# A macaron block on one core: the 7-product 2x2 block scheme in the first feed-forward as well

## The chip, the core and the metric

The kernel runs on one NeuronCore of a Trainium2 chip. The core has a matrix engine (PE, with a separate row PEld for its weight loads), a vector engine (DVE), a scalar engine (ACT), a general engine (POOL) and a queue engine (SP) that issues nearly all DMAs. Each engine works through its own list of instructions in order and waits on semaphores where an instruction needs another engine's result. The metric is the device time of one execution in microseconds (us).

## The reference, cut to what matters

One transformer-like layer on 256 tokens of 1024 features, in float32. Its first and last parts are feed-forward blocks of the same shape:

```python
def swiglu(h, w_in, w_down):              # h 256x1024, w_in 1024x5632, w_down 2816x1024
    gate, up = jnp.split(h @ w_in, 2, axis=-1)
    return (jax.nn.silu(gate) * up) @ w_down

h = rmsnorm(x, ffn1_pre_g[l])
x = x + 0.5 * rmsnorm(swiglu(h, ffn1_w_in[l], ffn1_w_down[l]), ffn1_post_g[l])
... # a gated linear recurrence, a causal attention, a cross-attention to a memory
h = rmsnorm(x, ffn2_pre_g[l])
x = x + 0.5 * rmsnorm(swiglu(h, ffn2_w_in[l], ffn2_w_down[l]), ffn2_post_g[l])
```

Only the order and the form in which `h @ w_in` is computed in the first block changes.

## The kernel before, in words

**Split products.** Every large product is made from two halves of each number: a rounded `hi` and the rest `lo = raw - hi`. A product takes three matmuls: hi by hi, hi by lo, lo by hi. So each weight tile of 128x1024 ("unit", 512 KB) is loaded into a buffer `raw` (four of them), ACT casts it to `hi` (L128) and DVE subtracts to get `lo` (L129); `hi` and `lo` have eight buffers each. A unit's load can start when a `raw` buffer is free, and its cast when a `hi`/`lo` pair is free.

**A feed-forward block** (`ffn`, L370 to L605) works through 11 chunks of 256 hidden columns. A chunk's projection has 4 weight units (512 columns, gate beside up) and, for each half of the tokens (`h`, 128 tokens), 8 blocks of 128 features by 3 matmuls: 48 matmuls of 128x512. `act_evac` then makes silu(gate)*up from PSUM (ACT L393/L395, DVE L401/L403). `flush` transposes a finished chunk on PE (L385) and splits it into `acts[c]`. `down(c, h)` multiplies it by 2 units of the down weight: 12 matmuls of 128x512 for a half, into four PSUM banks `acc`. Down products run one chunk or so behind the projections; the last three chunks' are left for the end (`STAG`). Then `post` normalises and adds, and the next stage begins.

**Where the two blocks differ.** The first block starts the kernel. Its chunks 0, 1 and 2 go through `act_first`, which uses each weight block for both token halves in turn, since the loads have only begun. The loads of the token matrix and of chunk 0's weights (`heads`, L611 to L616) use the four `raw` buffers and the two buffers `wide`. Its tokens `X1` carry no row scale; 1/rms enters in `act_evac` as `r2[h]`. The second block has tokens `X4` and at chunk 2 calls `mixed` (L265): `row_of` makes a row of the scales (two small matmuls on PE, L252), the tokens become full precision again and are multiplied by the row (`full`, L270 and L271), split anew (`N`), and four sums and differences of token blocks (`sums`, L280) are split as well. From chunk 3 on this block projects from `N`.

**`quad(c, done)`** (L408) computes two chunks together. The tokens are taken as 2x2 blocks (token half by even or odd feature block), the weights as 2x2 blocks (even or odd feature block by chunk), and the Winograd form of Strassen's scheme makes the 2x2 product with 7 block products in place of 8: 7 times 4 feature blocks times 3 matmuls, 84 in place of 96. In exchange DVE adds weight blocks (L436, L437, L439, L485) and both ACT and DVE split those sums (`two`, L414): 14 splits of 128x1024 for a pair of chunks in place of 8. The second chunk's raw weights go to `wide` (two buffers of two units). Four `down` calls stand between the products. In the kernel before, only the second block calls `quad`, for the pairs 5 with 6 and 8 with 9 (`QUADS`, L51 and L552).

**Buffers of one pool.** Token matrices, `acts`, `full`, `sums`, the weight sums (`sum`, L434) and the rows `grow` share a pool of 21 buffers of 4 KB per partition ("m4"). The next stage's token matrix `X2` (4 of them) is requested before the first block (L642).

**The order of the work** is made by a planner at build time. It reads the program in written order (that is the priority), keeps a simulated time for each engine, gives an engine the first instruction that is ready in its simulation, and gives buffers out as they come free. `after(n)` and `tc.issue_after` tie an instruction behind another one on its engine. On the chip the order of each engine, SP's included, is then fixed.

Of the kernel before, what the change touches and what calls it, by code (L numbers as in the profile page):

```python
# [16 lines left out]
P = 128  # L17
# [30 lines left out]

X_AT = 11

QUADS = (5, 8)  # L51


_ORDER = [
# [15 lines left out]
def block_kernel(ctx: ExitStack, tc: tile.TileContext, wts, head_in, gf_in, x_in, mem_in, memT_in, cols, rows, fbias, masks, out):  # L70
# [296 lines left out]
            queue.dma_start(out[h * P : (h + 1) * P, a:b], xh)  # L367


    def ffn(w_in, w_dn, X, r2, n_tok, i_row, first_half, second_half=None):  # L370

        acts = {}
        late = []
# [13 lines left out]

        mix = []

        def act_evac(ps, c, h):  # L390
# [5 lines left out]
            if c == NFF - 1 and h == 1 and not first_half:  # L396
                with tc.issue_after(silu.ins):
                    S.activation(warm, ones[:, 0:1], AF.Sqrt)
            a = sp.tile([P, FC], F32, tag="c1", name=nm("at"), bufs=7)
            if mix:  # L400
                V.tensor_tensor(out=a, in0=ps[:, FC:], in1=sg, op=ALU.mult)  # L401
            else:
                V.scalar_tensor_tensor(out=a, in0=ps[:, FC:], scalar=r2[h], in1=sg, op0=ALU.mult, op1=ALU.mult)  # L403
            ats[c, h] = a
            if (c, 1 - h) in ats:
                late.append(c)

        def quad(c, n_down):  # L408

            N, ((s1h, s1l), (s2h, s2l), (s3h, s3l), (s4h, s4l)) = mix[0]  # L410
            for k in (c, c + 1):
                acts[k] = m4([P, 2, 2, T], F32R, "act")

            def two(src):  # L414
                hi, lo = (p.rearrange("p (i n) -> p i n", i=2) for p in parts_of())
                split(hi, lo, src)
                return [(hi[:, i], lo[:, i]) for i in range(2)]

            B11, B21, wide, first, second_, fourth = ([] for _ in range(6))
            for q in range(2):  # L420
                W = wp.tile([P, 2, 2, 512], F32, tag="wide", name=nm("wide"), bufs=2)
                raws = []
                for i in range(2):
                    u = _AT[w_in] + 4 * c + 2 * q + i
                    raw = wp.tile([P, D], F32, tag="raw", name=nm("raw"), bufs=4)
                    loads.append(nc.sync.dma_start(raw, wts[u - 4]).ins)
                    loads.append(nc.sync.dma_start(W[:, i].rearrange("p j n -> p (j n)"), wts[u]).ins)
# [24 lines left out]
            def prod(ps, A, B, i, start, stop=False):  # L452
                (ah, al), (bh, bl) = A(i), B[i]
                MM(ps, ah, bh, start=start and i == 0, stop=False, skip_group_check=True)
                MM(ps, ah, bl, start=False, stop=False, skip_group_check=True)
                MM(ps, al, bh, start=False, stop=i == 3, skip_group_check=True)

            def prods(ps, A, B, start, stop=False):
                for i in range(4):
                    prod(ps, A, B, i, start, stop)  # L460

            def keep(ps):
                t = sp.tile([P, 512], F32, tag="z2", name=nm("keep"), bufs=3)
                S.copy(t, ps)
                return t

            b1, b2, b3 = mm(), mm(), trp()
# [4 lines left out]
            with tc.issue_after(summed):  # L472
                flush(n + L_ACT)
            p1 = keep(b1)
            prods(b2, F(s1h, s1l), T1, True)
            V.tensor_tensor(out=p1, in0=p1, in1=b3, op=ALU.add)
            act_evac(p1, c, 0)
            down(n_down, 0)
            T2 = two(second_[0]) + two(second_[1])
            prods(b1, F(s2h, s2l), T2, False)  # L480
            w = keep(b1)
            down(n_down, 1)
            T3 = []
# [6 lines left out]
            act_evac(v, c + 1, 1)  # L490
            down(n_down + 1, 0)
            T4 = two(fourth[0]) + two(fourth[1])
            prods(b1, X(1, 1), T4, False, True)
            act_evac(b1, c, 1)
            down(n_down + 1, 1)
            B22 = []
            for W in wide:
                B22 += two(W[:, :, 1])
            prods(b2, F(s4h, s4l), B22, False, True)
            V.tensor_tensor(out=w, in0=b2, in1=w, op=ALU.subtract)  # L500
            act_evac(w, c + 1, 0)

        def act_tok(c, h):
            ps = mm()
# [16 lines left out]
        def down(c, h, cols=((0, 512), (512, 1024))):  # L521
            act = acts[c]
            hs = slice(h * P, (h + 1) * P)
            for j in range(2):
                wh, wl = unit(w_dn, 2 * c + j)
                ah, al = act[:, 0, j, hs], act[:, 1, j, hs]
                for lo, up in cols:
                    for i, (a, w) in enumerate(((ah, wh), (ah, wl), (al, wh))):
                        MM(accs[h][lo // 512][:, lo % 512 : lo % 512 + up - lo], a, w[:, lo:up], start=(c == 0 and j == 0 and i == 0), stop=(c == NFF - 1 and j == 1 and i == 2))

        for c in range(n_tok):
            acts[c] = m4([P, 2, 2, T], F32R, "act")
        for h in range(2):
# [2 lines left out]
                act_tok(c, h)  # L536
            if h == 0 and n_tok:
                second_half(m)
        accs = None
        done = 0  # L540
        if callable(r2):
            outs = [act_first(c, acc) for c in range(2)]
# [6 lines left out]
        for c in range(n_tok, NFF):  # L549
            if c in acts:  # L550
                continue
            if not first_half and c in QUADS:  # L552
                quad(c, done)
                done += 2
                continue
# [7 lines left out]
            else:  # L563
                for h in range(2):
                    n = len(log)
                    act_tok(c, h)
                    if c == 2 or c > NFF - STAG + 1 or c - 2 in QUADS and not first_half:
                        flush(n + L_ACT)
            if c == NFF - 1:
                flush(n + L_ACT)  # L570
            if c == QUADS[0] - 3 and not first_half:
                mix.append(mixed(X, r2))
                X = mix[0][0]
            if c == (6 if first_half else 7):
# [6 lines left out]
            while done < min(c - 1, NFF - STAG):  # L581
                n = len(log)
                for h in range(2):
                    down(done, h)
                if first_half or c + 1 not in QUADS:
                    flush(n + L_ACT)
                done += 1
        left, right = (0, 512), (512, 1024)
        m = len(log)
        for cut in (left, right):  # L590
            for c in range(NFF - STAG, NFF):
                down(c, 0, (cut,))
        flush(m + L_ACT)
        post(accs[0], 0, grow, 0.5, not first_half)
        m = len(log)
        if first_half:
            for c in range(NFF - STAG, NFF):
                down(c, 1)
            first_half(m)
            post(accs[1], 1, grow, 0.5)  # L600
        else:
            for cut in (left, right):
                for c in range(NFF - STAG, NFF):
                    down(c, 1, (cut,))
            post_last(accs[1], 1, grow, 0.5)  # L605

# [32 lines left out]
            nc.sync.dma_start(fb_s, fbias)  # L639
# [620 lines left out]
```

## Time and profile before

| what | value |
| --- | --- |
| time, median of 3 runs | 795.22 us (795.21 to 795.88) |
| profiled execution, its own time | 795.3 us |
| profiled execution, its span of instructions | 793.5 us |
| PE busy | 784.3 us, 99% of the span |
| PEld, DVE, ACT busy | 86%, 71%, 55% |
| granted clock of PE, mean | 0.999 |
| bytes by DMA | 147.43 MB, mean 186 GB/s |

The profile page has six parts: busy time of each engine; the span in 40 slices of 19.8 us, with a digit for the busy tenths; DMA queues; the chain of work that ended last, followed back from the end; the costliest groups of instructions; DMA issues. Beside the page the trace answers views: windows (busy time of each engine in given stretches), a timeline of one engine (start, duration, engine, line, operation, tiles, count, and in brackets the idle time before it and what ended it), and the chain in order of time (start, length, what). All starts are us from the span's start. A matmul's busy time overlaps that of the next one, so the pace of matmuls is read from a stretch of the chain (length over count), not from an instruction's duration.

The first block runs from the start to about 192 us, the middle stages to about 602 us, the second block from there to the end.

### The profile page before, as it was taken

To read this page: it belongs to the slowest core of one execution; us is meant where nothing else is said; L and a number is where in the kernel's file an instruction comes from. 1 tells how busy PE (TensorE), PEld (TensorE's weight loads), DVE (VectorE), ACT (ScalarE), POOL (GpSimd) and SP (SyncE) were. 2 spreads that over 40 slices of the span, in tenths; PEclk is the share of its full clock that TensorE was granted. 3 is DMA by queue.
4 is the path that set the end of the run, shared out by engine and by line. 5 is a ranking of instruction groups with operands and counts; after the bars stand their busy time and mean duration, and the time that the engine had idled before them with its cause. 6 is when DMAs were issued, how large, how long until landed. Compare 5 with 4: busy or idle time off the path is not lost.

```text
span 793.5 us, 12866 instructions
## 1 busy us (share of the span) xinstructions
PE 784.3 (99%) x5048; PEld 679.2 (86%) x5048; DVE 565.0 (71%) x884; ACT 435.5 (55%) x659; POOL 9.2 (1%) x21
## 2 busy tenths in 40 slices
PE   9999999999999999999999999999999999999996
PEld 7888888888899999998888888999888888888885
DVE  6774545557767898578776665965758799978973
ACT  7654444546753446447675444754746655664751
POOL 0000000000000100100000000000000000000000
PEclk9999999999999999999999999999999999999999
DMA  9776755664555555653497755456454544473441
GB/s 347 250 256 207 220 194 159 189 209 160 162 184 143 178 174 157 211 195 120 141 313 270 234 172 198 137 183 212 133 176 143 185 161 163 162 256 113 154 159 53
DMA packets 43691, 147.43 MB, mean 186 GB/s; under 512 B 4840, under 2 KB 8304, under 8 KB 43632
## 3 DMA queue, kind: packets, MB, share of 16 engines
q1 hardware_dynamic: 43024, 144.92, 55.8%
q0 software_dynamic: 464, 1.58, 0.8%
q8 instruction: 39, 0.64, 0.3%
q14 instruction: 20, 0.16, 0.1%
q10 hardware_dynamic: 144, 0.13, 0.0%
HBM read 145.56 MB, written 1.06 MB: 185 GB/s over the span
## 4 chain that ended last, share of the span: by engine, by line
PE 98%; DMA 0%; DVE 0%; issue 0%; ACT 0%; DVEq 0%; ACTq 0%
PE mm L84 66%; PE acc L84 28%; PE tr L84 2%; PE tr L385 1%; PE tr L305 1%; DMA head<-in_head_dram 0%; PE tr L939 0%; PE tr L1028 0%; PE tr L1131 0%; DVEq L1258 0%; DVE xs L366 0%; DVE post L351 0%; ACT hi L629 0%; ACT hT L147 0%; ACT junk L234 0%
## 5 line engine op out<-in xcount | busy, mean ns | idle before, releaser
L129 DVE TENSOR_TENSOR lo<-raw,hi 128x1024 fp32r<-128x1024 f32 (+1 forms) x244 | 291.6, 1208 | 94.9 <-ACT hi L128 88.1
L128 ACT CAST hi<-raw 128x1024 fp32r<-128x1024 f32 (+1 forms) x244 | 249.3, 1037 | 138.8 <-PE mm L84 85.5
L84 PE MATMUL mm<-lo,hT 128*128 128x512 f32 (+1 forms) x544 | 208.6, 386 | 0.0
L84 PE MATMUL mm<-hi,hT 128*128 128x512 f32 (+1 forms) x544 | 208.4, 385 | 0.0
L84 PE MATMUL mm<-hi,lT 128*128 128x512 f32 (+1 forms) x544 | 207.3, 385 | 0.0
L84 PEld LDWEIGHTS mm<-hi,hT 128*128 128x128 f32 x544 | 102.2, 188 | 20.2 <-ACT hT L262 0.5
L84 PEld LDWEIGHTS mm<-hi,lT 128*128 128x128 f32 x544 | 102.1, 188 | 19.8 <-DVE lT L263 0.7
L84 PEld LDWEIGHTS mm<-lo,hT 128*128 128x128 f32 x544 | 102.0, 188 | 18.5
L84 PE MATMUL acc<-hi,act 128*128 128x512 f32 x352 | 112.7, 391 | 0.0
L84 PE MATMUL mm<-hT,hi 128*128 128x256 f32 x384 | 109.0, 284 | 0.1
L84 PE MATMUL mm<-hT,lo 128*128 128x256 f32 x384 | 109.0, 284 | 0.0
L84 PE MATMUL mm<-lT,hi 128*128 128x256 f32 x384 | 108.9, 284 | 0.0
L84 PEld LDWEIGHTS acc<-hi,act 128*128 128x128 f32 x352 | 66.1, 188 | 13.6 <-DVE act L148 0.2
L84 PEld LDWEIGHTS mm<-hT,hi 128*128 128x128 f32 x384 | 73.6, 192 | 0.4 <-issue 0.3
L84 PEld LDWEIGHTS mm<-hT,lo 128*128 128x128 f32 x384 | 73.6, 192 | 0.1
L84 PEld LDWEIGHTS mm<-lT,hi 128*128 128x128 f32 x384 | 73.6, 192 | 0.1
L84 PE MATMUL acc<-lo,act 128*128 128x512 f32 x176 | 69.6, 395 | 0.0
L84 PEld LDWEIGHTS acc<-lo,act 128*128 128x128 f32 x176 | 33.1, 188 | 6.4
L84 PE MATMUL acc<-hi,hT 128*128 128x512 f32 x96 | 35.6, 398 | 0.1
L84 PE MATMUL acc<-hi,lT 128*128 128x512 f32 x96 | 35.1, 392 | 0.0
L84 PE MATMUL acc<-lo,hT 128*128 128x512 f32 x96 | 34.9, 391 | 0.0
L395 ACT ACTIVATE sg<-mm,rstd 128x256 f32<-128x256 f32 x24 | 11.4, 476 | 36.6 <-PE mm L84 36.6
(233 smaller groups left out, 815.5 us busy)
## 6 DMA issues: line engine op xcount, KB each, us to landing
raw<-in_wts_dram SPq DMA_DIRECT2D x240, 512.0 KB, 4.5
raw<-in_gf_dram SPq DMA_DIRECT2D x12, 344.0 KB, 3.9
wide<-in_wts_dram SPq DMA_DIRECT2D x8, 512.0 KB, 6.0
head<-in_head_dram SPq DMA_DIRECT2D x8, 388.0 KB, 5.8
grow<-in_rows_dram SPq DMA_DIRECT2D x4, 512.0 KB, 6.0
xs<-in_x_dram SPq DMA_DIRECT2D x2, 512.0 KB, 8.6
cbm<-cd POOLq DMA_DIRECT2D x2, 512.0 KB, 7.9
brow<-in_rows_dram SPq DMA_DIRECT2D x4, 256.0 KB, 5.5
```

What stands on the lines that cost most here:

```text
L84: log.append(PE.matmul(*args, **kw).ins)
L128: S.copy(h, r)
L129: V.tensor_tensor(out=l, in0=r, in1=h.bitcast(F32), op=ALU.subtract)
L305: PE.transpose(ps[:, j * P : (j + 1) * P], src(kb), ident)
L385: PE.transpose(trv[:, j, h * P : (h + 1) * P], ats[c, h][:, j * P : (j + 1) * P], ident)
L395: silu = S.activation(sg, ps[:, :FC], AF.Silu, scale=r2[h])
```

## The change

A tuple of pairs is given to each block: `QUADS_1` for the first, `QUADS_2` for the second, both (5, 8). So the first block now also calls `mixed` at chunk 2, projects chunks 3 to 10 from `N`, and computes chunks 5 with 6 and 8 with 9 by `quad`. `X2` gets its buffers only at the end of the first block. The row `grow` is loaded at chunk 4 in both blocks (before: chunk 6 in the first, 7 in the second), since chunks 5 and 6 don't pass that line any more. The diff also adds branches for a pair that ends with the last chunk (`last`, `flush_half`, `done == NFF - 2`); with the pairs (5, 8) `quad` starts at 5 and 8, `NFF - 2` is 9, and none of them is taken. The branch `len(late) == 2` in `quad` isn't taken either: at both calls one finished chunk waits for its transposes.

```diff
-QUADS = (5, 8)
+QUADS_1 = (5, 8)
+QUADS_2 = (5, 8)
...
-    def ffn(w_in, w_dn, X, r2, n_tok, i_row, first_half, second_half=None):
+    def ffn(w_in, w_dn, X, r2, n_tok, i_row, quads, first_half, second_half=None):
...
+            if len(late) == 2:
+                flush(n + 4)
                 flush(n + L_ACT)
+            else:
+                with tc.issue_after(summed):
+                    flush(n + L_ACT)
...
-            if not first_half and c in QUADS:
+            if c in quads:
                 quad(c, done)
...
-                    if c == 2 or c > NFF - STAG + 1 or c - 2 in QUADS and not first_half:
+                    if c == 2 or c > NFF - STAG + 1 or c - 2 in quads:
                         flush(n + L_ACT)
...
-            if c == QUADS[0] - 3 and not first_half:
+            if quads and c == max(2, quads[0] - 3):
                 mix.append(mixed(X, r2))
                 X = mix[0][0]
-            if c == (6 if first_half else 7):
+            if grow is None and c >= 4:
                 grow = load_row(i_row)
...
-                if first_half or c + 1 not in QUADS:
+                if c + 1 not in quads:
                     flush(n + L_ACT)
...
-    X2 = Pair()
+    X2 = Pair(0)
...
-    ffn("f1_in", "f1_dn", X1, norm_1, 0, 0, lambda m: half(X2, r2, 0, G_MIX, m + L_F1))
+    def first(m):
+        X2.more()
+        X2.more()
+        half(X2, r2, 0, G_MIX, m + L_F1)
+
+    ffn("f1_in", "f1_dn", X1, norm_1, 0, 0, QUADS_1, first)
...
-    ffn("f2_in", "f2_dn", X4, r4, 2, 3, None, second)
+    ffn("f2_in", "f2_dn", X4, r4, 2, 3, QUADS_2, None, second)
```

More of the change, by code (lines that the diff above doesn't have):

```diff
@@ L388, in ffn, with flush_half @@
         mix = []
+        def flush_half(c, h, n):
+            trv = trp().rearrange("p (j t) -> p j t", j=2)[:, :, :P]
+            hs = slice(h * P, h * P + P)
+            with after(n):
+                for j in range(2):
+                    PE.transpose(trv[:, j], ats[c, h][:, j * P : (j + 1) * P], ident)
+                split(acts[c][:, 0, :, hs], acts[c][:, 1, :, hs], trv)
         def act_evac(ps, c, h):
@@ L395, in act_evac @@
                 silu = S.activation(sg, ps[:, :FC], AF.Silu, scale=r2[h])
-            if c == NFF - 1 and h == 1 and not first_half:
+            if c == NFF - 1 and (c, 1 - h) in ats and not first_half:
                 with tc.issue_after(silu.ins):
@@ L465, in keep @@
                 return t
+            last = c == NFF - 2
             b1, b2, b3 = mm(), mm(), trp()
@@ L471, in quad @@
                 prod(b3, X(0, 1), B21, i, True, True)
-            with tc.issue_after(summed):
+            if len(late) == 2:
+                flush(n + 4)
                 flush(n + L_ACT)
+            else:
+                with tc.issue_after(summed):
+                    flush(n + L_ACT)
             p1 = keep(b1)
@@ L481, in quad @@
             w = keep(b1)
+            n = len(log)
             down(n_down, 1)
+            if last:
+                flush_half(c, 0, n)
             T3 = []
@@ L490, in quad, with fourth_product, third_product @@
             act_evac(v, c + 1, 1)
+            n = len(log)
             down(n_down + 1, 0)
[L492 to L501, printed above, removed]
+            def fourth_product():
+                T4 = two(fourth[0]) + two(fourth[1])
+                prods(b1, X(1, 1), T4, False, True)
+                act_evac(b1, c, 1)
+            def third_product():
+                B22 = two(wide[0][:, :, 1]) + two(wide[1][:, :, 1])
+                prods(b2, F(s4h, s4l), B22, False, True)
+                V.tensor_tensor(out=w, in0=b2, in1=w, op=ALU.subtract)
+                act_evac(w, c + 1, 0)
+            if last:
+                down(n_down + 1, 1)
+                flush_half(c + 1, 1, n + L_ACT)
+                third_product()
+                n = len(log)
+                fourth_product()
+                flush_half(c + 1, 0, n + 12)
+            else:
+                fourth_product()
+                down(n_down + 1, 1)
+                third_product()
         def act_tok(c, h):
@@ L528, in down @@
                     for i, (a, w) in enumerate(((ah, wh), (ah, wl), (al, wh))):
-                        MM(accs[h][lo // 512][:, lo % 512 : lo % 512 + up - lo], a, w[:, lo:up], start=(c == 0 and j == 0 and i == 0), stop=(c == NFF - 1 and j == 1 and i == 2))
+                        MM(accs[h][lo // 512][:, lo % 512 : lo % 512 + up - lo], a, w[:, lo:up], start=(c == 0 and j == 0 and i == 0), stop=(c == (NFF - 2 if h and quads and quads[-1] == NFF - 2 else NFF - 1) and j == 1 and i == 2))
         for c in range(n_tok):
@@ L538, in ffn @@
                 second_half(m)
-        accs = None
+        accs = grow = None
         done = 0
@@ L589, in ffn @@
         m = len(log)
[L590 to L593, printed above, removed]
+        if done == NFF - 2:
+            for k in (NFF - 2, NFF - 1):
+                for cut in (left, right):
+                    down(k, 0, (cut,))
+            flush_half(NFF - 2, 1, m + L_Y)
+        else:
+            for cut in (left, right):
+                for c in range(done, NFF):
+                    down(c, 0, (cut,))
+            flush(m + L_ACT)
         post(accs[0], 0, grow, 0.5, not first_half)
         m = len(log)
+        ends = (NFF - 1, NFF - 2) if done == NFF - 2 else range(done, NFF)
         if first_half:
-            for c in range(NFF - STAG, NFF):
+            for c in ends:
                 down(c, 1)
@@ L602, in ffn @@
             for cut in (left, right):
-                for c in range(NFF - STAG, NFF):
+                for c in ends:
                     down(c, 1, (cut,))
```

## The prediction

> **What bounds the kernel now.** I read the page first: busy time, then the slices.
>
> ```profile
> PE 784.3 (99%) x5048; PEld 679.2 (86%) x5048; DVE 565.0 (71%) x884; ACT 435.5 (55%) x659; POOL 9.2 (1%) x21
> PE   9999999999999999999999999999999999999996
> PEclk9999999999999999999999999999999999999999
> DMA  9776755664555555653497755456454544473441
> ```
>
> PE has work in every slice but the last, at full clock. So a matmul that goes should shorten the span by its pace, as long as what feeds PE keeps up. Next I read the chain in order of time, in the first block and in the second, which already does what the first is to do.
>
> ```profile
> 39.43 5.03 PE acc L84 x22
> 45.36 10.91 PE mm L84 x48
> ...
> 191.78 3.09 PE mm L84 x13
> ...
> 639.95 0.45 PE tr L84 x4
> ...
> 645.43 0.44 PE tr L385 x4
> ...
> 685.47 2.76 PE mm L84 x12
> ...
> 771.54 14.86 PE acc L84 x65
> 786.40 0.02 issue
> ```
>
> 48 matmuls take 10.91 us: 0.2273 us each. From the end of chunk 2 the first block takes 191.78 - 39.43 = 152.35 us. It has 8 chunks of 48 and 11 down products of 24 there, 648 matmuls, 147.3 us; nine chunks' transposes at 0.44 add 4.0, the next stage's eight some 0.9: 152.2. The second block takes 786.40 - 639.95 = 146.45 us for 624 matmuls (141.8), nine transposes (4.0) and `row_of` (the row at 639.95, 0.45): 146.3. Both sums close within 0.2 us, so the block with pairs has no idle PE in it. That is the main evidence: the same order of work, on the same buffers, already runs at PE's pace.
>
> **The change part by part.** *Removed on PE*: two pairs, 12 matmuls each, 24 x 0.2273 = 5.46 us. A rule can be set against the row here. In the Trainium skill, TensorE: Matmul & The Clock Gate, section "Wait — 56ns, not 53.3ns?", a warm matmul of 512 columns starts 215.7 ns after the last; by that figure the 24 would be worth an estimated 5.18 us. The trace differs (227.3 ns), and I go by the trace.
>
> *Added on PE*: `row_of`, 0.45 us. Base of the sum: -5.46 + 0.45 = -5.01 us, if nothing waits. It is also the most that can be gained; no PE idle time stands in the first block that could go besides.
>
> *Added on DVE and ACT at chunk 2: `mixed`.* Its price stands in DVE's timeline of the second block.
>
> ```profile
> 641.01 0.47 DVE L403 SCALAR_TENSOR_TENSOR at<-mm,rstd,sg 128x256 f32<-128x256 f32 x1
> 641.40 2.35 DVE L270 TENSOR_TENSOR full<-hT,lT 128x1024 f32<-128x1024 f32 x2
> 643.67 2.36 DVE L271 TENSOR_TENSOR full<-full,row 128x1024 f32<-128x1024 f32 x2
> 645.94 1.22 DVE L129 TENSOR_TENSOR lo<-raw,hi 128x1024 fp32r<-128x1024 f32 x1
> 647.07 1.22 DVE L148 TENSOR_TENSOR lT<-full,hT 128x1024 fp32r<-128x1024 f32 x1
> 649.34 1.22 DVE L148 TENSOR_TENSOR lT<-full,hT 128x1024 fp32r<-128x1024 f32 x1
> 650.48 0.76 DVE L280 TENSOR_TENSOR sums<-full 128x256 f32<-128x256 f32 x2
> 655.43 1.23 DVE L148 TENSOR_TENSOR sl<-sums,sh 128x1024 fp32r<-128x1024 f32 x1
> ```
>
> 2.35 + 2.36 + 2 x 1.22 + 4 pairs at 0.76 + 2 x 1.23 = 12.7 us of DVE. PE needs the first part, `N`, at chunk 3: lo of its first half ends at 647.07 + 1.22 = 648.29, 8.3 us after chunk 2's end at 639.95. PE covers 0.45 + 5.5 + 0.4 with `row_of`, down(0) and transposes, then takes products of N's hi and some of down(1). In the first block DVE is later. The rows of its chunk 2:
>
> ```profile
> 40.24 0.48 DVE L403 SCALAR_TENSOR_TENSOR at<-mm,rstd,sg 128x256 f32<-128x256 f32 x1
> 42.08 0.48 DVE L403 SCALAR_TENSOR_TENSOR at<-mm,rstd,sg 128x256 f32<-128x256 f32 x1
> 42.70 1.23 DVE L129 TENSOR_TENSOR lo<-raw,hi 128x1024 fp32r<-128x1024 f32 x1
> ```
>
> The second `at` ends at 42.56, 3.1 us after chunk 2's end (39.43, where down(0) starts); in the second block it is 641.48 - 639.95 = 1.5. So `N` comes about 1.6 us later against PE. Besides, DVE is a unit behind (the split at 42.70 is down(1)'s first, done in the second block before `mixed`), 1.2 us. So 2.8 us of lag, and the filler down(1) isn't there yet. Stall of PE at chunk 3: lower end 0 (`full`'s additions put between the two `at`, as the planner may), upper end 2.8. I take 0.6, near the lower end, because `N`'s hi and 8 matmuls with it (1.8 us) come before its lo.
>
> *Added on DVE in a pair*: 6 more splits of 128x1024 (at 1.22: 7.3 us), 12 additions of weights (4 of 128x1024 at 1.2, 8 of half the size at an estimated 0.7, half of 1.2 and a little: 10.4 us), 3 of products at the same 0.7. Near 20 us a pair. Windows tell whether DVE bears it:
>
> ```profile
> 30.00:60.00 30.00, 30.00 (x140) 24.80 (x139) 22.16 (x24) 17.71 (x22) 0.00 (x0) 1.00 0.78 254
> 60.00:90.00 30.00, 30.00 (x138) 24.82 (x137) 15.16 (x16) 13.94 (x17) 0.00 (x0) 1.00 0.60 184
> 640.00:670.00 30.00, 30.00 (x139) 24.68 (x138) 28.82 (x36) 15.82 (x21) 0.00 (x0) 1.00 0.49 166
> 670.00:700.00 30.00, 30.00 (x136) 24.84 (x135) 27.75 (x31) 20.70 (x24) 0.00 (x0) 1.00 0.47 151
> ```
>
> Columns after the length: PE, PEld, DVE, ACT, POOL busy, clock, DMA share, GB/s. DVE has 28.82 and 27.75 of 30 us at chunks 3, 4 and the first pair, ACT at most 20.70, and PE stays at 30.00. How far ahead DVE is there:
>
> ```profile
> 678.98 1.23 DVE L148 TENSOR_TENSOR lo<-sum,hi 128x1024 fp32r<-128x1024 f32 x1
> 684.65 1.23 DVE L148 TENSOR_TENSOR lo<-sum,hi 128x1024 fp32r<-128x1024 f32 x1
> ```
>
> The first ends at 680.2 and PE uses that sum in the second half of the twelve from 685.47, at 686.8: 6.6 us ahead; the later sums are as early or earlier. A lag of 2.8 us leaves 3.8. Price of DVE's work in the pairs: 0; its cover gone, each us of lag beyond 6.6 is a us of PE. ACT's extra casts lie within its free third: 0.
>
> *Loads of `wide`.* This step is moved most. SP's rows of the second block:
>
> ```profile
> 410.24 0.33 SPq L427 DMA_DIRECT2D wide<-in_wts_dram  x1
> ...
> 658.78 4.03 SPq L426 DMA_DIRECT2D raw<-in_wts_dram  x4
> ```
>
> The pair's `raw` loads go out at 658.78, but its first `wide` load at 410.24: the planner issues it when the buffer is free. In the first block `wide` is freed by `heads`, and DVE's last work on those ends at 13.7 us (the row behind SP's):
>
> ```profile
> 11.89 0.35 SPq L639 DMA_DIRECT2D fb_s<-in_fbias_dram  x1
> 15.53 60.62 SPq L127 DMA_DIRECT2D raw<-in_wts_dram  x28
> ```
>
> ```profile
> 13.23 0.48 DVE L263 SCALAR_TENSOR_TENSOR lT<-head,hT 128x256 fp32r<-128x256 f32 x1
> ```
>
> So I expect the four `wide` loads of pair 5 with 6 on SP between 11.89 and 15.53, ahead of chunk 2's `raw` loads, in a stretch where DMA is full:
>
> ```profile
> 13.19 1.05 ACT L128 CAST hi<-raw 128x1024 fp32r<-128x1024 f32 x1 [0.26 <-DMA raw<-in_wts_dram]
> 14.46 1.05 ACT L128 CAST hi<-raw 128x1024 fp32r<-128x1024 f32 x1 [0.22 <-DMA raw<-in_wts_dram]
> 21.97 1.04 ACT L128 CAST hi<-raw 128x1024 fp32r<-128x1024 f32 x1
> ```
>
> ```profile
> 16.00:20.00 4.00, 4.00 (x20) 3.30 (x19) 3.40 (x4) 3.49 (x7) 0.00 (x0) 1.00 1.03 400
> 24.00:28.00 4.00, 4.00 (x19) 3.30 (x19) 2.58 (x4) 1.83 (x4) 0.00 (x0) 1.00 0.53 148
> ```
>
> ```profile
> 27.61 4.99 PE mm L84 x22
> ```
>
> Units land 1.27 us apart (14.46 - 13.19), so four make 5.1 us. Chunk 2's first cast begins at 21.97 and would begin about 27, its lo end 2.3 us later, near 29.3; PE starts chunk 2 at 27.61 and wants the first lo after about four matmuls, at 28.5. The next units then come every 1.3 us and PE takes one every 2.7, and DMA has room from 24 on (0.53), so the delay shrinks by itself. Stall at chunk 2: lower end 0 (the loads fall behind chunk 2's), upper end 1.1 (29.3 against 28.5, and a cast behind ACT's silu of chunk 1). I take 0.2, near the lower end, since the row at 21.97 shows no wait for its load and so some slack. In the Trainium skill, DMA: Bandwidth & Descriptors, section "Queues, rings and completion order", descriptors of a ring are consumed in ring order; by that rule chunk 2's loads can't overtake the four, and the sum keeps the 0.2; if they shared the engines with them instead, it would be nearer the 1.1.
>
> *Edits with one answer.* `grow` two or three chunks earlier: one load of 512 KB among loads that are ready 6 us before use: 0 in both blocks (bounds -0.2 to +0.3; without that cover its place on SP costs 1.3). `X2` late: its first writer stands at the block's end, where the pairs' buffers are free: 0. `raw` loads of the pairs move past down units in SP's order as in the second block: 0. The end of the block: DVE catches up there in the second block, so the next stage's units are up to 1 us late at worst; taken 0.
>
> **Sum**: -5.01 + 0.6 + 0.2 = -4.2 us. The profiled execution is 795.3 us (span 793.5 and 1.8 around it), so 791.1; it lies 0.08 above the median of 795.22, so against the runs 791.0.
>
> **The rivals.** With S for PE's total wait, the time is 790.2 + S. A difference from before below 0.2% (1.6 us) can't be told from none.
>
> *Everything is covered* (S under 0.3): 790.3. For it: PE never waits in the second block. Against: 2.8 us less lead.
>
> *The first pair starves for a while* (S from 2 to 3.4): 792.2 to 793.6. DVE is busy for 56.6 of the 60 us from 640 on, so lag from the start is hardly regained before the pair's end; against it are the 6.6 us of lead.
>
> *The delays cancel the gain* (S from 3.4 to 6.6): 793.6 to 796.8, no change to be told.
>
> *Slower: DVE becomes the bound from the start to the first pair.* The place is chunk 3 to the pair. The lag would have to pass 6.6 + 5.0 = 11.6 us; four `wide` loads (5.1 us), a start at 2.8, and a `mixed` of 12.7 that isn't overlapped with casts could give 13 to 16, so S near 8: 798. Against: 30 to 90 us has 60 - 37.3 = 22.7 us of free DVE, `mixed` needs 12.7 of it, and the 0.53 shows DMA regaining. In the Trainium skill, TensorE: Matmul & The Clock Gate, section "What's actually happening", PE falls to half clock after an idle window of about 3.4 us; by that rule one long stall would cost an estimated 1.7 us more, 799.7; no run here shows it, every window above has 1.00.
>
> **How the numbers follow.** Chances: all covered 0.2; forecast (S 0.3 to 2.0, 790.5 to 792.2) 0.48; first pair starves 0.16; cancelled 0.06; slower 0.10. Faster 0.84, same 0.06, slower 0.10. The time is the forecast's, 791.0. The range goes from 789.9 (all covered, and `grow` at its better bound) to 793.5, the end of the third case; what is left out is 0.16 and a little.
>
> **What would show it.** PE's instructions 5048 - 24 + 4 = 5028. The first block from chunk 2's end near 147.3 + S. SP: `wide` between 12 and 16 us. DVE over 28 of 30 us somewhere in 40 to 100, PE 30.00 there. Stalls, if any, on PE's weight loads behind DVE's lT or lo at 27 to 30 and 44 to 49 us. Wrong would be: gaps of PE within the pairs (79 to 107), a wait of SP for a pool buffer, or a changed order after 190 us that costs elsewhere.

## The result and the profile after

The changed kernel takes 790.65 us (median of 4 runs, 790.08 to 791.19) against 795.44 for the kernel before on the same chip (4 runs, 795.21 to 795.88): a ratio of 0.9939, interval 0.9922 to 0.9956. The profiled execution took 791.19 us, of which the span is 789.3.

The page after, busy time and slices (the rows answer to those of before):

```profile
PE 779.5 (99%) x5028; PEld 674.5 (85%) x5028; DVE 609.5 (77%) x944; ACT 451.5 (57%) x682; POOL 9.3 (1%) x21
...
DVE  6798989978766898578685665965758799978963
```

PE has 5028 instructions as worked out, 4.8 us less of busy time, and is still the bound. DVE has 44.5 us more work (565.0 before). The chain in order of time, after:

```profile
39.28 5.87 DMA raw<-in_wts_dram
...
45.23 1.05 ACT hi L129
46.28 0.95 ACT hT L148
...
47.28 1.20 PE mm L85 x4
...
86.59 2.76 PE mm L85 x12
...
188.52 3.09 PE mm L85 x13
```

From 80 us on the first block's chain is PE alone, its pairs (the rows at 86.59 and on) without an interruption; the next stage begins at 188.52 where it was 191.78. Ahead of chunk 3 the chain leaves PE: a load, a cast of a weight on ACT, then ACT's cast of `N`. What PE waited for, in total, after:

```profile
PE tr L85 <- DVE ones L198: 1.1, 1, 1.1
PE mm L85 <- ACT hT L148: 0.9, 1, 0.9
PE acc L85 <- ACT hT L263: 0.6, 1, 0.6
```

The first wait is the start of the kernel, there before as well. The second is chunk 3's (0.86 us, at 47.28). The third is at 8.64 us, where a part of the token matrix landed late in this execution; a second profile of the same kernel, `rep_after`, has none there. Before, the same view had one other row, which is gone after:

```profile
PE acc L84 <- issue: 0.7, 1, 0.7
```

It stood at 294 us, far behind the change. So the two spans compare like this: -5.46 for 24 matmuls, +0.45 `row_of`, +0.86 at chunk 3, +0.59 at the start, -0.69 at 294 us: -4.25. Measured: 793.46 to 789.33, -4.13; 0.12 is left over.

The windows after (columns as in the prediction), the last line from 70 us:

```profile
30.00:60.00 30.00, 29.14 (x137) 23.88 (x136) 26.92 (x34) 18.53 (x24) 0.00 (x0) 1.00 0.67 233
60.00:90.00 30.00, 30.00 (x138) 24.82 (x137) 26.65 (x31) 16.62 (x20) 0.00 (x0) 1.00 0.66 233
...
70.00:100.00 30.00, 30.00 (x136) 24.84 (x135) 29.04 (x33) 19.03 (x23) 0.00 (x0) 1.00 0.45 165
```

DVE goes from 22.16 and 15.16 us to 26.92 and 26.65, and has 29.04 of 30 around the first pair; PE loses 0.86 us in the first window and nothing in the others.

### The profile page after: what moved, and what is told of

It is laid out like the page before. It is cut to its first block, busy times and chain, and to the rows that moved or that the text cites. A ratio compares the mean times of both kernels' runs of the same rounds, so it can differ in the third digit from the quotient of the medians.

```text
span 789.3 us, 12909 instructions
## 1 busy us (share of the span) xinstructions
PE 779.5 (99%) x5028; PEld 674.5 (85%) x5028; DVE 609.5 (77%) x944; ACT 451.5 (57%) x682; POOL 9.3 (1%) x21
## 4 chain that ended last, share of the span: by engine, by line
PE 95%; DMA 2%; ACT 1%; DVE 1%; issue 0%; DVEq 0%; SPq 0%; ACTq 0%
PE mm L85 64%; PE acc L85 27%; PE tr L85 3%; DMA raw<-in_wts_dram 1%; PE tr L386 1%; PE tr L306 1%; DMA head<-in_head_dram 1%; ACT hi L129 0%; DVE lo L130 0%; PE tr L983 0%; PE tr L1072 0%; PE tr L1175 0%; ACT hT L148 0%; DVEq L1302 0%; SPq L655 0%
## 5 line engine op out<-in xcount | busy, mean ns | idle before, releaser
L130 DVE TENSOR_TENSOR lo<-raw,hi 128x1024 fp32r<-128x1024 f32 (+1 forms) x228 | 271.6, 1207 | 68.4 <-ACT hi L129 64.1
L129 ACT CAST hi<-raw 128x1024 fp32r<-128x1024 f32 (+1 forms) x228 | 232.2, 1036 | 127.0 <-PE mm L85 76.7
L85 PE MATMUL mm<-hi,hT 128*128 128x512 f32 (+1 forms) x496 | 189.7, 385 | 0.9 <-ACT hT L148 0.9
L85 PE MATMUL mm<-lo,hT 128*128 128x512 f32 (+1 forms) x496 | 190.2, 386 | 0.0
L85 PE MATMUL mm<-hi,lT 128*128 128x512 f32 (+1 forms) x496 | 188.5, 385 | 0.0
L85 PEld LDWEIGHTS mm<-hi,hT 128*128 128x128 f32 x496 | 93.1, 188 | 19.5 <-ACT hT L148 1.6
L85 PEld LDWEIGHTS mm<-hi,lT 128*128 128x128 f32 x496 | 93.1, 188 | 17.7 <-DVE lT L264 0.7
L85 PEld LDWEIGHTS mm<-lo,hT 128*128 128x128 f32 x496 | 93.0, 188 | 16.5
L148 ACT CAST hi<-sum 128x1024 fp32r<-128x1024 f32 x24 | 24.6, 1051 | 19.1 <-DVE sum L446 15.1
```

Source lines behind the costliest of these rows:

```text
L85: log.append(PE.matmul(*args, **kw).ins)
L129: S.copy(h, r)
L130: V.tensor_tensor(out=l, in0=r, in1=h.bitcast(F32), op=ALU.subtract)
L148: S.copy(hi, src)
```

## Experiments

The kernels ran in three groups, each with runs of the kernel before beside it: the first group (`rep_before`, `rep_after`, `mix3`, `wide_early`) with 795.39, the second (`mix_only`, `pair8`, `x2_early`, `three2`) with 795.34, the third (`after3`, `x2_again`, `cast_held`, `warm18`) with 795.54. Times are medians; "after" is the changed kernel, run again as `rep_after` (790.89) and `after3` (791.33).

**Does the gain repeat?** Both kernels again, without an edit.

> The kernel before once more, for what one execution's profile leaves to chance. Theory 1 (the start is chance, the gap at 294 us belongs to the program's order): PE waits again for 0.6 to 0.7 us near 294 us, in the middle stages, and PE's wait for the first loads differs by up to 0.6 us from the first profile. Theory 2 (both are chance): the gap at 294 us is gone or elsewhere.

> The changed kernel once more. Theory 1: the wait of PE at chunk 3 (0.86 us near 47 us, for the cast of N) stands again within 0.2 us, the wait near 8.6 us at the start is anything from 0 to 0.6 us, no gap near 290 us; 790.1 to 791.2 us. Theory 2: the wait at chunk 3 comes and goes like the start's.

Measured: 795.14 (one run, span 793.3) and 790.89 (789.90 to 791.35; ratio 0.9943, 0.9930 to 0.9955). `rep_before` has the gap near 294 us again (0.60), `rep_after` the wait at chunk 3 again (1.02) and no gap. The gain and both details repeat.

**Where does the wait at chunk 3 come from?** The rows of ACT and DVE in front of it, after. ACT:

```profile
45.23 1.05 ACT L129 CAST hi<-raw 128x1024 fp32r<-128x1024 f32 x1 [1.13 <-DMA raw<-in_wts_dram]
46.19 1.04 ACT L148 CAST hT<-full 128x1024 fp32r<-128x1024 f32 x1
```

DVE, the addition that makes the first half of `N` ready:

```profile
42.53 1.23 DVE L272 TENSOR_TENSOR full<-full,row 128x1024 f32<-128x1024 f32 x1 [1.14 <-ACT row L255]
```

`N`'s first half is ready at 43.76 (42.53 + 1.23), yet ACT casts it only at 46.19. Ahead of it in ACT's list stands the cast of down(1)'s second unit, whose load lands at 45.2, and ACT works through its list in order. DVE isn't what PE waits for. The length of the wait goes with that landing. The same two rows in `after3`, the same program:

```profile
44.02 1.05 ACT L129 CAST hi<-raw 128x1024 fp32r<-128x1024 f32 x1 [1.20 <-DMA raw<-in_wts_dram]
44.97 1.04 ACT L148 CAST hT<-full 128x1024 fp32r<-128x1024 f32 x1
```

There PE waits 0.42 us. Seven profiles have this wait (after, `rep_after`, `after3`, and below `x2_early`, `x2_again`, `three2` and `warm18`), from 0.19 to 1.23 us, and in every one of them chunk 3's first matmul starts 2.12 or 2.13 us after that load has landed. Two experiments take the wait away in different ways.

*`mixed` one chunk later in the first block* (`mix3`):

```diff
-            if quads and c == max(2, quads[0] - 3):
+            if quads and c == (3 if first_half else max(2, quads[0] - 3)):
```

> The first block calls mixed at chunk 3 in place of chunk 2; all else as in the changed kernel. Theory 1 (PE's wait is DVE's lag at chunk 2, where weights have just begun to arrive): at chunk 3 DVE has caught up, the 0.86 us go, and the time is 0.6 to 1.0 us below the changed kernel's, near 789.8. Rival (mixed costs PE a wait wherever it stands, since 12.7 us of DVE come at once; or the pair then starves, its sums being ready one chunk later): 0 to +3 us against the changed kernel, with waits of PE at chunk 4 or in the first pair.

Measured: 789.82 us (789.18 to 790.84), ratio 0.9935 (0.9921 to 0.9948). No wait at chunk 3; 1.07 below `rep_after`, whose wait there is 1.02. By its median it is the fastest of all that were run; the interval of its ratio overlaps that of `rep_after`. That agrees with theory 1's number, but not with its reason: moving `mixed` takes it away from the late load as well as from DVE's backlog, so this run alone can't tell the two apart. Its window from chunk 4 to the first pair:

```profile
60.00:90.00 30.00, 30.00 (x137) 24.69 (x136) 30.00 (x41) 16.52 (x20) 0.00 (x0) 1.00 0.48 174
```

DVE is busy for all 30 us and PE for all 30 too: a full DVE is no wait by itself.

*The cast held back* (`cast_held`): ACT may cast down(1)'s second unit only after `N`'s first cast.

```diff
...
+            if (name, i) in held:
+                with tc.issue_after(held[name, i]):
+                    cache[u] = load_split(wts[u - 4])
...
-            split(N.h[q], N.l[q], full[q])
+            cast = split(N.h[q], N.l[q], full[q])
+            if q == 0:
+                held.setdefault(("f1_dn", 3), cast)
```

> As the changed kernel, with one cast tied: ACT casts the second weight unit of down(1) behind the first cast of N, not ahead of it. Theory 1 (PE's wait at chunk 3 is ACT's order: the cast of N stands behind the cast of a weight that lands late): the first product of chunk 3 no longer waits over 0.3 us, and 0.6 to 1.0 us go against the changed kernel of these runs, near 790.0. Rival (it is DVE's lag, as the prediction had it): the wait stays within 0.2 us of the changed kernel's.

Measured: 792.68 us (790.88 to 793.50), ratio 0.9963 (0.9950 to 0.9975): 1.35 above `after3`, with intervals that overlap. ACT in `cast_held`:

```profile
42.29 1.05 ACT L153 CAST hT<-full 128x1024 fp32r<-128x1024 f32 x1
...
46.09 1.05 ACT L153 CAST hT<-full 128x1024 fp32r<-128x1024 f32 x1 [1.80 <-DVE full L278]
52.53 1.05 ACT L130 CAST hi<-raw 128x1024 fp32r<-128x1024 f32 x1 [5.39 <-DMA raw<-in_wts_dram]
53.49 1.04 ACT L153 CAST sh<-sums 128x1024 fp32r<-128x1024 f32 x1
```

The first cast of `N` comes at 42.29 and chunk 3 starts without a wait: the cause is confirmed. The other half of theory 1, 0.6 to 1.0 us less time, failed. The next late load, chunk 4's first unit (cast at 52.53, after at 50.58), holds the casts behind it, and PE, now ahead, runs into what it had not met before. The edit also moved a load: the fourth `wide` load goes out at 40.01, ahead of that unit, and after at 46.85, behind it. So the lost time isn't the price of the order of casts alone. PE's timeline of `cast_held` in the first pair, and DVE's sum before the first of the waits:

```profile
84.61 0.40 PE L85 MATMUL mm<-hi,sh 128*128 128x512 f32 x1
...
91.45 0.50 PE L85 MATMUL mm<-lo,sh 128*128 128x512 f32 x1 [0.79 <-DVE lo L154]
...
97.83 0.50 PE L85 MATMUL mm<-hi,sh 128*128 128x512 f32 x1 [0.75 <-ACT keep L482]
...
104.00 0.50 PE L85 MATMUL mm<-hi,hT 128*128 128x512 f32 x1 [0.43 <-ACT keep L482]
```

```profile
90.18 1.22 DVE L154 TENSOR_TENSOR lo<-sum,hi 128x1024 fp32r<-128x1024 f32 x1
```

How thin the lead is in the changed kernel itself can be read off. DVE's later sums there:

```profile
82.75 1.23 DVE L149 TENSOR_TENSOR lo<-sum,hi 128x1024 fp32r<-128x1024 f32 x1
...
89.12 1.22 DVE L149 TENSOR_TENSOR lo<-sum,hi 128x1024 fp32r<-128x1024 f32 x1
```

and PE's uses, then ACT's copy that frees the bank for the third product:

```profile
92.14 0.39 PE L85 MATMUL mm<-lo,sh 128*128 128x512 f32 x1
...
97.35 0.39 PE L85 MATMUL mm<-hi,sh 128*128 128x512 f32 x1
```

```profile
96.10 0.57 ACT L474 COPY keep<-mm 128x512 f32<-128x512 f32 x1
```

The second sum of the first product ends at 83.98, about 3.9 us ahead of its use (86.59 + 1.3). The second product's ends at 90.34 and is used at 92.14: 1.8 us. The copy ends at 96.67 for a use at 97.35: 0.7 us. (In `rep_after` these two are 2.3 and 1.2 us.) In `cast_held` PE reaches the pair 1.8 us earlier (its first product of sums begins at 84.61, after 86.43; 0.6 of this is the wait at 8.64 us, which `cast_held` has not) and DVE's sum comes 1.1 later (90.18 against 89.12), together more than 1.8, and the wait follows.

**Was the place of the `wide` loads wrong, and what would they have cost where the prediction put them?** SP after:

```profile
12.48 0.35 SPq L678 DMA_DIRECT2D fb_s<-in_fbias_dram  x1
16.11 23.50 SPq L128 DMA_DIRECT2D raw<-in_wts_dram  x12
39.66 1.54 SPq L437 DMA_DIRECT2D wide<-in_wts_dram  x3
...
46.85 0.43 SPq L437 DMA_DIRECT2D wide<-in_wts_dram  x1
```

They go out at 39.66 and 46.85, behind chunk 2's loads, not between 12 and 16. Why the planner put them there no view tells. `wide_early` puts the four where they were expected:

```diff
...
+        with tc.issue_after(fb_last):
+            for q in range(2):
+                W = wp.tile([P, 2, 2, 512], F32, tag="wide", name=nm("wide"), bufs=2)
+                for i in range(2):
+                    nc.sync.dma_start(W[:, i].rearrange("p j n -> p (j n)"), wts[_AT["f1_in"] + 4 * QUADS_1[0] + 2 * q + i])
+                early.append(W)
...
```

> The four wide loads of the first pair are written right behind the start's small loads, so that they stand on the queue ahead of chunk 2's weights, where the prediction had put them and the profile of the changed kernel has not (it has them near 40 us). By the prediction's step: chunk 2's weights land 5.1 us later and PE waits 0 to 1.1 us there; with the DMA less loaded at 40 to 52 us nothing else changes, so 0 to +1.1 us against the changed kernel. Rival (the lead at the start is all there is, and the delay is passed on from chunk to chunk): +3 to +5 us, with waits of PE at chunks 2 and 3 of over 3 us.

Measured: 795.44 us (794.48 to 796.02), ratio 1.0001 (0.9992 to 1.0010): 4.55 above `rep_after`, the whole gain. SP in `wide_early`, then the larger of PE's waits behind the start:

```profile
13.60 4.13 SPq L686 DMA_DIRECT2D wide<-in_wts_dram  x4
18.71 24.72 SPq L129 DMA_DIRECT2D raw<-in_wts_dram  x13
```

```profile
PE mm L85 <- ACT hi L130: 1.6, 1, 1.6
...
PE mm L85 <- ACT keep L477: 0.8, 1, 0.8
PE mm L85 <- ACT hT L149: 0.7, 1, 0.7
```

and ACT there:

```profile
27.86 0.84 ACT L406 ACTIVATE sg<-acc,rstd 128x256 f32<-128x256 f32 x2 [3.17 <-PE acc L85]
28.59 3.89 ACT L130 CAST hi<-raw 128x1024 fp32r<-128x1024 f32 x4
```

Chunk 2's loads land from 26.90 on instead of 20.92 (`rep_after`). By then ACT stands at the silu of chunk 1, which needs PE, and the casts come behind it, at 28.59. Matched matmul by matmul with `rep_after`, PE is 2.65 us later after chunk 2 (0.38 of it from the kernel's start), 3.4 after chunk 3, 4.5 in the first pair and 5.2 at the block's end: the delay isn't made up, later stages add to it. So the total is the rival's (+3 to +5), though its waits of over 3 us at chunks 2 and 3 are 1.64 and 1.21 here. By the Trainium skill, DMA: Bandwidth & Descriptors, section "Queues, rings and completion order", each DMA engine consumes the descriptors of a ring in ring order; the trace agrees, the four `wide` loads land from 21.4 to 25.6 and chunk 2's after them.

**One part at a time.** `mixed` without any pair in the first block (`mix_only`):

```diff
-QUADS_1 = (5, 8)
+QUADS_1 = ()
...
-            if quads and c == max(2, quads[0] - 3):
+            if c == 2:
```

> The first block calls mixed at chunk 2 and projects chunks 3 to 10 from N, but has no pair. Theory 1 (the sum of the prediction): the cost of mixed alone against the kernel before is 0.45 us for row_of and 0.9 to 1.0 us of wait at chunk 3, so +1.3 to +1.5 us if the 0.6 us gap at 294 us stays and +0.7 to +0.9 if it goes: 796.1 to 796.9 us. Rival (the gain does not come from the 24 matmuls alone, but the new order and the scaled tokens give something too): 795.4 us or less.

Measured: 796.03 us (795.47 to 796.84), ratio 1.0010 (1.0001 to 1.0019): +0.69, just below theory 1's range, whose wait at chunk 3 didn't come, though `mixed` stands where it does after. ACT in `mix_only`:

```profile
43.91 1.05 ACT L129 CAST hi<-raw 128x1024 fp32r<-128x1024 f32 x1 [0.46 <-DMA raw<-in_wts_dram]
44.87 1.04 ACT L148 CAST hT<-full 128x1024 fp32r<-128x1024 f32 x1
```

The load in question landed at 43.83 here; 2.12 us later is 45.95, and PE came to chunk 3 at 46.12. It took 4.96 us from issue to landing, with no `wide` load behind it. Without one it took 4.96 to 5.45 us in five profiles (5.07 before, 5.41 `rep_before`, 5.45 `pair8`), with three or four behind it 4.90 to 6.37 in eight (5.87 after, 6.37 `rep_after`, 5.10 `x2_early`, 4.90 `cast_held`). The longest are among those with `wide` loads behind, but the two groups overlap, so that these loads delay it isn't shown.

The second pair alone (`pair8`), with `mixed` at chunk 5:

```diff
-QUADS_1 = (5, 8)
+QUADS_1 = (8,)
```

> The first block has one pair only, 8 with 9, and so calls mixed at chunk 5. Theory 1: 12 matmuls at 0.2273 us less and row_of, -2.73 + 0.45 = -2.3 us, with no wait of PE at chunk 6, since DVE has caught up by then; with the 0.6 us gap at 294 us gone -2.9, so 792.5 to 793.1 us. Rival (a pair is worth more or less than its matmuls, by waits inside it): outside 792.2 to 793.4.

Measured: 792.80 us (792.48 to 793.70), ratio 0.9970 (0.9958 to 0.9981): -2.54, where 12 matmuls less `row_of` make -2.28. PE's waits in its profile are all at the start, besides the gap near 293 us. A pair is worth what its matmuls are worth.

**Do the next stage's buffers, taken late, matter?** `X2` as before (`x2_early`, and the same program again as `x2_again`):

```diff
-    X2 = Pair(0)
+    X2 = Pair()
...
-        X2.more()
-        X2.more()
```

> The next stage's token buffers are requested before the first block, as in the kernel before; pairs as in the changed kernel. Theory 1 (buffers are given out at a tile's first use, so that requesting early holds nothing): the same time as the changed kernel within 0.4 us, no new wait. Rival (four of 21 buffers are held through the block, where the pairs need some 20): PE waits in the first pair for weight sums that had no buffer, +2 us or more.

> The changed kernel on the same chip as the next three. Theory 1 (PE's wait at chunk 3 belongs to this program): 0.8 to 1.1 us of wait near 47 us, as twice before, and 790.7 to 791.0 us. Rival (it depends on how the loads happen to land): a wait of 0.2 us or less.

> The kernel with the next stage's buffers requested early, once more, beside the changed kernel on one chip. Theory 1 (requesting late neither gains nor costs; the 0.9 us less of the first run came from a weight load that landed at 44.2 in place of 45.2 us): its wait at chunk 3 and its time lie within 0.4 us of the changed kernel's in these runs, whatever they are. Rival (early is better by itself): 0.6 us or more below the changed kernel again, near 790.0.

Measured: 790.01 us (ratio 0.9935, 0.9921 to 0.9948) beside the second set of before; 790.75 (0.9943, 0.9930 to 0.9955) beside `after3` with 791.33 (0.9949, 0.9936 to 0.9963). None of the expectations fits: the wait in `after3`, 0.42, lies between its two cases, and `x2_again` differs from it by 0.81 us in the wait and 0.58 in the time, more than theory 1 allows and less than the rival. But the intervals overlap, and by the profiles the wait at chunk 3 was 0.19 us in `x2_early` and 1.23 in `x2_again`, the same program, so a difference this small can be that wait's chance. The buffers limit nothing that can be told.

**Where does DVE become the bound?** Three pairs in a row in the second block, where before and after have two with chunk 7 between them (`three2`):

```diff
-QUADS_2 = (5, 8)
+QUADS_2 = (4, 6, 8)
```

> The second block has three pairs in a row, 4 with 5, 6 with 7 and 8 with 9, in place of two with chunk 7 between; the first block is as in the changed kernel. It tests how much DVE's lead of some 6.6 us bears. Theory 1 (DVE has near 36 us of work in a pair of 31 us of PE, so each further pair in a row takes 5 us of the lead): 2.73 us of matmuls go, and waits of 3 to 8 us come in the second and third pair, so 0 to +6 us against the changed kernel. Rival (PE stays the bound): -2.7 us, 788.2 us.

Measured: 796.65 us (794.42 to 799.12), ratio 1.0017 (1.0007 to 1.0027), though 12 matmuls fewer (2.7 us) than after. Windows, then PE's waits, of `three2`:

```profile
690.00:720.00 30.00, 27.09 (x118) 20.79 (x117) 29.20 (x34) 19.49 (x26) 0.00 (x0) 1.00 0.45 146
720.00:750.00 30.00, 27.42 (x120) 21.12 (x119) 29.66 (x35) 16.61 (x22) 0.00 (x0) 1.00 0.53 181
```

```profile
PE mm L85 <- DVE lo L149: 4.3, 6, 1.4
```

PE loses 5.5 us in 60, most of it behind DVE's splits of sums. DVE has 29.20 of 30 us here and 30.00 in `mix3`, and only here does PE wait. How far ahead DVE is tells the two apart. The second sum of a pair's first product in `three2`, on DVE in the first pair and at its use on PE in the second:

```profile
662.73 1.21 DVE L149 TENSOR_TENSOR lo<-sum,hi 128x1024 fp32r<-128x1024 f32 x1
```

```profile
698.41 0.50 PE L85 MATMUL mm<-lo,sh 128*128 128x512 f32 x1 [0.61 <-DVE lo L149]
```

In the first pair it ends 1.8 us ahead of its use at 665.76; in the second and third PE waits for it, 0.61 and 0.62 us. In `mix3`, with one pair and then a chunk without sums, it ends at 82.46, 3.5 us ahead of its use at 85.97.

**What is the gap at 294 us?** It is 0.69 us before, 0.60 in `rep_before`, 0.62 in `pair8`, 0.11 in `mix_only`. Counting PE's matmuls and weight loads together it comes when 4289 have started (4290 in `pair8`) in all four, within the run of 16-column matmuls of the recurrence (`acc<-q,k`). After and in the other profiles without the gap, with 20 or 32 matmuls fewer than before, the 4289th falls among the 256-column matmuls, and there is no gap. `warm18` gives the changed kernel 20 instructions more, at the very start, by more and narrower warm-up matmuls:

```diff
-    for _ in range(WARM):
-        MM(wps[:, :P], ones, ones, start=True, stop=True)
+    for _ in range(WARM + 10):
+        MM(wps[:, :56], ones, ones[:, :56], start=True, stop=True)
```

> The start's 8 warm-up products of 128 columns are replaced by 18 of 56 columns: 20 matmul instructions more, 5048 as in the kernel before, in the same time of PE. Theory 1 (the gap near 294 us of the kernel before stands at a place in PE's list of instructions, the 4289th, and only shows where short matmuls run there): a gap of 0.5 to 0.8 us near 290 us comes back, +0.4 to +0.8 us against the changed kernel. Rival (it belongs to the code around it, or to chance): no gap of over 0.2 us between 280 and 300 us, and the same time within 0.3 us.

Measured: 796.75 us (795.44 to 798.01), ratio 1.0016 (1.0007 to 1.0024), 5.4 above `after3`. The gap is back. PE's timeline in `warm18`, the start and the gap:

```profile
1.07 7.93 PE L85 MATMUL tr<-ones 128*128 128x56 f32 x36 [1.07 <-DVE ones L198]
8.77 1.20 PE L85 MATMUL acc<-hi,hT 128*128 128x512 f32 x2
9.77 1.05 PE L85 MATMUL acc<-hi,lT 128*128 128x512 f32 x2
...
295.73 0.32 PE L85 MATMUL acc<-q,k 128*32 128x16 f32 x17 [0.47 <-issue]
```

and in `after3`:

```profile
1.06 3.78 PE L85 MATMUL tr<-ones 128*128 128x128 f32 x16 [1.06 <-DVE ones L198]
4.80 0.89 PE L85 MATMUL acc<-hi,hT 128*128 128x512 f32 x2
```

The gap is worth 0.6 us of the time; most of the rest is the experiment's own flaw. The 36 narrow warm-ups take 0.22 us each, the 16 wide ones 0.24, so the real work starts 3.97 us later (8.77 against 4.80), and the time missed what was expected (+0.4 to +0.8). Matmul by matmul against `after3`: +3.97 at the first, +4.63 from some ten matmuls on, +5.2 after chunk 3 (its wait is 0.98 here, 0.42 there), +5.8 at the block's end, +5.9 by 292 us and +6.5 behind the gap, which is the spans' difference (795.0 and 788.5). The total says nothing on the gap; the place and the step from 5.9 to 6.5 do.

## Why the prediction was right

The time was 790.65 us for 791.0, inside the range, and the case was the forecast's: PE's wait came to 0.4 to 1.0 us in three profiles where 0.8 was put. The matmuls and `row_of` were rightly worked out. That the waits fit as well is in part luck: one of the two that were put in the sum has another cause, the other isn't there, and a gap that no step had went away.

*The matmuls removed and `row_of`*: right. 5028 instructions; the pairs' twelve take 2.72 us as in the second block. The block from chunk 2's end (39.89, where `row_of` begins in PE's timeline) to 188.52 takes 148.6 us; 147.3 with the wait of 0.86 is 148.2. Of the 0.4 left, some 0.16 is that a timeline's starts lie ahead of the chain's (39.27 for 39.43 before); the rest is not placed. `mix_only` with +0.69 and `pair8` with -2.54 give each part alone. That 227.3 ns and not 215.7 is a matmul's price here can't be told from totals that vary by 1 us.

*The stall at chunk 3*: the size was right (0.6 put, 0.86, 1.02 and 0.42 measured), the mechanism wrong. The step that failed is "so 2.8 us of lag, and the filler down(1) isn't there yet", which laid the stall on DVE. DVE had `N`'s first half in full precision ready at 43.76, 3.9 us after chunk 2's end and 2.7 before PE came to chunk 3; the planner had put the addition for it (at 39.17) even ahead of the first `at`. PE waited for `N`'s hi, not its lo, and hi was late because ACT's list has a weight's cast in front whose load lands late. The upper end, 2.8 us, was not a bound of this mechanism at all: the delay is as long as a load is late. That the size fits is luck.

*The `wide` loads*: the step "I expect the four `wide` loads of pair 5 with 6 on SP between 11.89 and 15.53" failed. It read the second block's rule (issued when the buffer is free) into the first; three of the loads went out from 39.66 on and the fourth at 46.85. So the 0.2 us at chunk 2 are 0. The bound beside it failed as well: with the loads at that place the cost is 4.55 us, not at most 1.1. "The delay shrinks by itself" was argued from the DMA's free share; it left out that casts which miss their turn stand behind ACT's silu, and that a stage without slack, `mixed` and the first pair, came next. The prediction came out right here because its two errors didn't meet.

*DVE's work in the pairs*: price 0, right in the kernel as it is; 29.04 of 30 us around the pair with PE at 30.00. For the first product the number fits: a lead of 6.6 less 2.8 was to leave 3.8, and 3.9 is there. But the 2.8 came from the lag at chunk 3 that the runs don't show, so the fit is no proof of the working. "The later sums are as early or earlier" holds in the second block, where it was read (the second product's first sum ends at 683.61 for a use at 691.02), and failed in the first: there it is 1.8 us ahead, and ACT's copy for the third 0.7. The margin for more delay was 0.7 to 1.8 us, not 3.8; `cast_held` fell into it and paid 1.97 us of waits in the pair. DVE's added work was 44.5 us, below the 52.7 that the steps add up to (12.7 and twice near 20).

*`grow`, `X2`, the order of `raw` loads, the block's end*: 0, as far as the runs can tell; the view of PE's waits after lists none behind 47.28 us. One thing behind the change did move: the gap at 294 us went, 0.6 to 0.7 us, which no step had. It cancelled most of the wait at chunk 3.

*The rivals.* "Everything is covered" is what `mix3` reaches: 789.82 for 790.3, the gap's 0.6 taken off. "The first pair starves" didn't come about after, but it is what `cast_held` shows, at 792.68 for 792.2 to 793.6. "The delays cancel the gain" is `wide_early`, at 795.44, by the cause that was named for the slower case, the four loads. DVE as the bound came about only with three pairs in a row (`three2`). The clock rule that was cited for one long stall wasn't tried: no wait of PE behind its first instruction lasts over 1.64 us in any profile.

## What to carry to other kernels

Read a stall's cause from the list of the engine that releases it, row by row: a critical cast can stand behind a cast that is waiting for its load, and then neither engine is short of time; moving the work by a chunk took the wait away here. A busy share of 100% on a helper engine doesn't tell whether it binds (`mix3` 30.00 with no wait, `three2` 29.20 with 2.9 us lost); the lead of each result over its use does, and it has to be read for every use, the copies out of PSUM too. And before a place in the order is carried over from another stage, ask what else has to be true there, then price the case that it is wrong with the stages that follow, not with the first one alone.

## What the runs showed of the hardware

**A gap of PE at a fixed place of its instruction list.** Before, PE's timeline has this row:

```profile
294.13 0.32 PE L84 MATMUL acc<-q,k 128*32 128x16 f32 x15 [0.69 <-issue]
```

It comes when 4289 or 4290 matmuls and weight loads have started, in all five profiles that have it, 0.11 to 0.69 us long, when that place falls among matmuls that start every 10 ns or so (113 in 1.16 us before the gap); it was not seen when it falls among 256-column ones at 120 ns. That looks like a supply of instructions that short matmuls outrun, but no row shows what PE waited for, so it is an inference. A change of 20 instructions can give or take 0.6 us this way, 300 us from where it was made.

**Narrow warm-ups do not go faster, and the full pace came later behind them.** Warm-up matmuls with 56 columns started 0.21 us apart, as those with 128 columns did (but for the last of these in `mix3` and `pair8`, 0.11 apart). After 7.93 us of the narrow ones, the first six matmuls of 512 columns in `warm18` still started 0.43 us apart (the first two 0.57), near twice the 0.227 of later ones, until 11.47 us, though the granted clock is 1.00 in the record. With the wide ones the count of such slow matmuls goes from none (`mix3`, `x2_again`) to five (`x2_early`), and they end by 7.04 us at the latest, in 13 profiles. By the Trainium skill, TensorE: Matmul & The Clock Gate, section "What's actually happening", some 3.4 us of sustained work bring the full clock, and a matmul of 512 columns takes 426.7 ns without it (section "Wait — 56ns, not 53.3ns?"). The pace agrees with the second figure; the time doesn't agree with the first in the one profile with narrow warm-ups, and the measurement decides. Why wasn't tried.

**The same load lands 4.90 to 6.37 us after its issue.** One load of 512 KB, down(1)'s second unit, varies that much over 13 profiles, and by 1.2 us between two executions of one program (5.10 in `x2_early`, 6.31 in `x2_again`). What sets it, no run shows.
